# Storing the softmax reciprocals as rows, fixed bias places, scaling o in place, and other DMA queues in an encoder layer

## The chip, the cores and the metric

The kernel runs on one core of a Trainium2 chip. A core has five engines: TensorE (PE in the profile, with its weight loads as PEld), VectorE (DVE), ScalarE (ACT), GpSimd (POOL) and SyncE (SP), which only issues DMAs here. Each engine takes its instructions in order. SyncE and GpSimd each feed a DMA queue of their own (q1 and q0 in the profile), and both queues are served by the same 16 DMA engines. The metric is the time of one execution on the device in microseconds; less is better.

## The reference

One layer of a streaming encoder is computed for two groups of frames: a prompt of 1024 frames and 64 further frames of a running stream (the sample), which has 512 cached rows of keys and values. All is float32.

```
proj = rmsnorm(x, g_mix) @ w_in              # columns: cb cc ch | q k v | ga gb
cv   = causal depthwise conv, width 3, of cc*ch
ya   = (cb * cv) @ w_conv_out
o    = softmax(q k^T / 8 + bias, over the own chunk of 64 and the 8 before) @ v   # 8 heads of 64
yb   = o @ w_attn_out
x    = x + (sigmoid(ga)*ya + sigmoid(gb)*yb) @ w_out
x    = x + (silu(n @ w1) * (n @ w3)) @ w2    # n = rmsnorm(x, g_ffn)
y    = rmsnorm(x, g_final)
```

The outputs are y for both groups, the last two inputs of the convolution, and the key and value rows to be kept.

## The kernel before, in words

**Numbers.** A float32 operand is split into two parts (`split`, L119): ScalarE casts the high part (L121) and VectorE subtracts it (L122). A product is three matmuls, high by high, high by low and low by high. Large products use seven block products in place of eight (`run`, L218).

**Frames.** The 1088 frames are kept in two halves of 544: 512 prompt frames and 32 sample frames each. Attention works on tiles of 128 prompt frames (t = 0 to 7) and one tile of the 64 sample frames (t = 8).

**Normalization and v** (L337 to L506). Nine tiles of frames are loaded in the order of `ORDER` (sample first), normalized, turned on TensorE (L405) and multiplied with the weights of v. The loads of the first two tiles and of these weights stand on SP's queue. The row `gm` (L374) holds the gains of the norm, turned by TensorE and copied by ScalarE; no tile can be scaled (L391) without it. `put_v` splits v and stores it per head to `v_d`, on Pool's queue.

**Projection units** (L476 to L738). Each unit is 256 columns of `w_in`. The list `units` sets the order. A unit's results go to DRAM scratch: `q_d`, `k_d`, `gb_d`, and `u_d` for cb times the convolution. While the first units run, four tiles of cached keys and values are loaded, turned and stored (`cache_tile`, L666).

**Attention beside gates** (L742 to L972). The rest of ga and gb, 12 blocks of 128 columns in `GATES`, are plain products, cut in 4 pieces of 272 frames (`gate`, L751): 24 matmuls of 128x272 a piece. Each piece is copied by ScalarE into one of two buffers (L759) and stored (L760). Attention is a generator of 75 steps: a step does the scores of one tile (`scores`, L822), the turning of the tile two steps back (`transposed`) and, for every second tile, the values of the tile three steps back (`values`). After each gate piece `between` (L931) lets some steps run: `PER` of them on average. Pieces 0 and 1 of the first four gates run without attention. The constant `LAST` says how many gates are left when attention must be through. The instructions of one engine are ordered by the compiler's planner, which moves them by its own model of times, so the order on SP is not strictly that of the code.

For each head `head_load` (L766 to L789) loads keys, queries (two copies of each of two parts), values and a bias tile, about 3 MB. The bias tile is 128 by 640; two corners of it are set to -1e30 by VectorE after the load (L787, L788). In `softmax` one VectorE instruction adds the bias and finds the row's maximum (L795), and ScalarE takes the exponential with the row sum (L805). `combine` (L807) adds the two parts of the values and stores o, not yet divided by the row sum, to `o_d` (L816, L820) from `co`, which has two buffers. At t = 8 VectorE takes the reciprocals of a head's sums (L847, L848), and Pool stores them to `rc_d` (L850, L853) from a tile in which partition p holds the value of frame p of each tile:

```python
nc.gpsimd.dma_start(
    rc_d[h, e * HT : e * HT + 512].rearrange("(t p) -> p t", p=P), sm[:, 4 * e : 4 * e + 4]
)
```

**Merge** (L949 to L998). With the last gate, for each k of four, u and o are loaded, and rc is spread over the 64 partitions of its head; VectorE multiplies o by rc (L967) and `split` writes the operand `ob`. The tiles of o (`ol`) and rc have one buffer each. Then for each of 8 blocks of columns come ya and yb, the sigmoids, and the sum of both.

**The rest** (L1000 on): output projection, second norm, feed-forward part and final norm. The change touches nothing there.

Of the kernel before, what the change touches and what calls it, by code (L numbers as in the profile page):

```python
# [8 lines left out]
F32 = mybir.dt.float32  # L9
# [24 lines left out]
HN = HT // 2  # L34
KB = [2, 3, 3, 3]
C_CB, C_CC, C_CH, C_Q, C_K, C_V, C_GA, C_GB = 0, 512, 1024, 1536, 2048, 2560, 3072, 4096
PER = 2.1
LAST = 1


class Quarters:
# [23 lines left out]
def encoder_kernel(ctx: ExitStack, tc: tile.TileContext, ins, outs):  # L65
# [40 lines left out]
    def bias_rows(h, a, n):  # L106
        return spread(ins["bias_ext"][h, a : a + n], n)
# [226 lines left out]
    def bank1(tag, nm):  # L334
        return ps1.tile([P, 2, 512], F32, tag=tag, name=nm, bufs=2)

    def put_v(st, src, n, row):  # L337
        st = st.bitcast(F32R).rearrange("p (h l d) -> p h l d", h=NH, l=2)
        s = src.rearrange("p (h d) -> p h d", h=NH)
        split(st[:n, :, 0, :], st[:n, :, 1, :], s[:n])  # L340
        nc.gpsimd.dma_start(
            v_d[:, row : row + n, :].rearrange("h t e -> t h e"),
            st[:n].rearrange("p h l d -> p h (l d)").bitcast(F32),
        )
# [9 lines left out]
    wv_raw = [rpool.tile([P, 4, ATT], F32, tag="raw", name=f"wv{half}") for half in range(2)]  # L354

    def load_wv(k0):
        nc.sync.dma_start(
            wv_raw[k0 // 4][:, k0 % 4 : k0 % 4 + 2],
            w_in[k0 * P : (k0 + 2) * P, C_V : C_V + ATT].rearrange("(k p) n -> p k n", p=P),
        )  # L360

    load_x(ORDER[0])
    load_wv(0)
    load_x(ORDER[1])
    load_wv(2)
    load_wv(4)
    load_wv(6)
# [6 lines left out]
    act.activation(gm, gp, AF.Copy, scale=-0.5)  # L374

    wv = []

# [77 lines left out]
    def v_tile(i):  # L455
        t0, n = TT[i]
        pv = bank1("BD", f"pvv{i}")[:, 0]
        for k in range(KD):
            if i == 8:
                a, b = xs8[:, k, :TS], xs8[:, k, TS:]  # L460
            else:
                a, b = xn.at(0, k, column(i), P), xn.at(1, k, column(i), P)
            mm(pv[:n], a, wv[k][0], start=k == 0, stop=False)
            mm(pv[:n], a, wv[k][1], start=False, stop=False)
            mm(pv[:n], b, wv[k][0], start=False, stop=k == KD - 1)
        put_v(slot(VST, D), pv, n, t0 if t0 < TP else TP + CACHE)
        if t0 >= TP - CACHE:
            v32 = scr[:, SQ : SQ + ATT]
            act.copy(v32[:n], pv[:n])
            if t0 < TP:  # L470
                dst = outs["cache_v_prompt"][t0 - (TP - CACHE) : t0 - (TP - CACHE) + n]
            else:
                dst = outs["cache_v_sample"][CACHE - TS :]
            nc.gpsimd.dma_start(dst, v32[:n])

    units = []  # L476
    for nm, u in (
        ("q", 0), ("q", 1), ("k", 0), ("k", 1), ("cc", 0), ("ch", 0), ("cb", 0), ("cc", 1), ("ch", 1), ("cb", 1),
        ("gb", 0), ("gb", 1),
    ):  # L480
        base = {"q": C_Q, "k": C_K, "cc": C_CC, "ch": C_CH, "cb": C_CB, "gb": C_GB}[nm]
        units.append((nm, u, w_in[:, base + 2 * u * P : base + 2 * (u + 1) * P]))
# [183 lines left out]
    def cache_tile(i):  # L666
        ct = cts[i]
        a = 0 if i else TS
        row = i * P + a - TS
        for nm, o in (("k", 0), ("v", ATT)):  # L670
            nc.gpsimd.dma_start(outs[f"cache_{nm}_sample"][row : row + P - a], ct[a:, o : o + ATT])
        put_v(slot(CC, 2 * ATT), ct[:, ATT:], P, TP + i * P)
        pk = bank1("BD", f"ckp{i}")[:, 0]
        for hp in range(4):
            nc.tensor.transpose(pk[:, hp * P : (hp + 1) * P], ct[:, hp * P : (hp + 1) * P], ident)
        st = slot(CC, 2 * ATT).bitcast(F32R).rearrange("p (l a t) -> p l a t", l=2, a=4)
        split(st[:, 0], st[:, 1], pk.rearrange("p (a t) -> p a t", a=4))
# [73 lines left out]
    def gate(i, cs):  # L751
        g, m = GATES[i]
        dst = ga_d if g == "a" else gb_d
        for c in cs:
            o, n = PIECES[c]
            ps = pmm.tile([P, 512], F32, tag="mm", name=f"g{i}_{c}")
            product(ps[:, :n], gate_w[i], xn, o, n)
            st = st_pool.tile([P, HN], F32, tag="st", name=f"gst{i}_{c}")
            act.copy(st[:, :n], ps[:, :n])  # L759
            nc.sync.dma_start(dst[m * P : (m + 1) * P, o : o + n], st[:, :n])  # L760

    gate_w = {}

    heads, sums = {}, {}

    def head_load(h):  # L766
        k = hd_pool.tile([P, TP], F32R, tag="k", name=f"kd{h}")
        nc.sync.dma_start(k.bitcast(F32), k_d[h, :, :, :TP].rearrange("l d t -> (l d) t"))
        q = []
        for l in range(2):  # L770
            qq = hd_pool.tile([P, T], F32R, tag=f"q{l}", name=f"qd{h}_{l}")
            for j in range(2):
                nc.sync.dma_start(qq[j * HD : (j + 1) * HD].bitcast(F32), q_d[h, l])
            q.append(qq)
        ks = hd_pool.tile([P, CACHE + TS], F32R, tag="ks", name=f"ksd{h}", bufs=1)
        nc.sync.dma_start(ks.bitcast(F32), k_d[h, :, :, TP:].rearrange("l d t -> (l d) t"))
        v = hd_pool.tile([P, 8, P], F32R, tag="v", name=f"vd{h}")
        nc.sync.dma_start(v.bitcast(F32), v_d[h, :TP].rearrange("(b p) e -> p b e", p=P))
        vs = hd_pool.tile([P, 5, P], F32R, tag="vs", name=f"vsd{h}", bufs=1)
        nc.sync.dma_start(vs[:, :4].bitcast(F32), v_d[h, TP : TP + CACHE].rearrange("(b p) e -> p b e", p=P))  # L780
        nc.sync.dma_start(vs[:TS, 4].bitcast(F32), v_d[h, TP + CACHE :])
        b = hd_pool.tile([P, 640], F32, tag="b", name=f"bias{h}")
        nc.sync.dma_start(b[:, :384], bias_rows(h, 0, 384))
        nc.sync.dma_start(
            b[:, 384:], bias_d[h, 127 : 127 + P * 383].rearrange("(p n) -> p n", n=383)[:, :256]
        )
        vec.memset(b[HD:, :HD], NEG)  # L787
        vec.memset(b[:HD, 576:], NEG)  # L788
        heads[h] = (q, k, ks, v, vs, b)  # L789

    def softmax(s, ps, bias, sm, nm):
# [15 lines left out]
    def combine(h, pv, n, tok, nm):  # L807

        a = at_pool.tile([HD, 2, 256], F32, tag="cmb_a", name=f"ca{nm}", bufs=1)
        o = at_pool.tile([HD, 256], F32, tag="cmb_o", name=f"co{nm}")  # L810
        act.copy(a[:, :, :n], pv[HD:])
        vec.tensor_tensor(a[:, :, :n], pv[:HD], a[:, :, :n], op=ALU.add)
        vec.tensor_tensor(o[:, :n], a[:, 0, :n], a[:, 1, :n], op=ALU.add)
        if tok < TP:
            c = tok if tok < 512 else HT + tok - 512
            nc.sync.dma_start(o_d[h * HD : (h + 1) * HD, c : c + n], o[:, :n])  # L816
        else:
            for e in range(2):
                c = 512 + e * HT
                nc.sync.dma_start(o_d[h * HD : (h + 1) * HD, c : c + 32], o[:, 32 * e : 32 * e + 32])  # L820

    def scores(h, t):  # L822
# [14 lines left out]
        b0 = 640 - n if t < 8 else 0  # L837
        if t == 0:
            sums[h] = at_pool.tile([P, 9], F32, tag="sm", name=f"sm{h}")
        sm = sums[h]  # L840
        softmax(
            s[:r, :n], ps[:r, :, :w] if parts == 2 else ps[:r, 0, :w], bias[:r, b0 : b0 + n], sm[:r, t : t + 1],
            f"{h}_{t}",
        )
        if t == 8:

            vec.reciprocal(sm[:, :8], sm[:, :8])  # L847
            vec.reciprocal(sm[:TS, 8:], sm[:TS, 8:])  # L848
            for e in range(2):
                nc.gpsimd.dma_start(  # L850
                    rc_d[h, e * HT : e * HT + 512].rearrange("(t p) -> p t", p=P), sm[:, 4 * e : 4 * e + 4]
                )
                nc.gpsimd.dma_start(  # L853
                    rc_d[h, e * HT + 512 : e * HT + HT].rearrange("(p t) -> p t", t=1), sm[32 * e : 32 * e + 32, 8:]
                )
        return s

    pts = {}
# [1 line left out]
    def transposed(h, t, s):  # L860
        tp = patt.tile([P, 2, 512], F32, tag="att", name=f"t{h}_{t}").rearrange("p a b -> p (a b)")
        if t == 8:
# [6 lines left out]
            split(pt[:, 0, :4, :], pt[:, 1, :4, :], tp[:, : 4 * TS].rearrange("p (b t) -> p b t", t=TS))  # L869
            split(pt[:TS, 0, 4, :], pt[:TS, 1, 4, :], tp[:TS, 512 : 512 + TS])  # L870
            pts[h, 4] = pt
            return
        g, j = divmod(t, 2)
        if j == 0:
# [72 lines left out]
    for i in range(4, len(GATES)):  # L947
        gate_w[i] = next_w()
        if i == len(GATES) - LAST:  # L949
# [6 lines left out]
            mp = pg_stack.enter_context(tc.tile_pool(name="mgp", bufs=4, reuse_waits="tile"))  # L956
            for k in range(4):
                nc.sync.dma_start(u.t[:, :, k].bitcast(F32), u_d[k])
                t = mp.tile([P, T], F32, tag="ol", name=f"ol{k}", bufs=1)
                nc.sync.dma_start(t, o_d[k * P : (k + 1) * P])  # L960
                r = mp.tile([P, T], F32, tag="rc", name=f"rc{k}", bufs=1)
                for j in range(2):
                    src = rc_d[2 * k + j]
                    nc.sync.dma_start(
                        r[j * HD : (j + 1) * HD], bass.AP(tensor=src.tensor, offset=src.offset, ap=[[0, HD], [1, T]])
                    )
                vec.tensor_tensor(t, t, r, op=ALU.mult)  # L967
                split(ob.t[:, 0, k], ob.t[:, 1, k], t)
        for c in range(4):
            gate(i, (c,))  # L970
            between()
# [575 lines left out]
```

## Time and profile before

| | |
|---|---|
| median of 3 runs | 1606.53 us (1606.35 to 1609.5) |
| profiled execution | 1621.55 us, span 1619.6 us |
| busy in the span | PE 1505.9 us (93%), DVE 984.9 (61%), ACT 682.8 (42%), POOL 101.2 (6%) |
| DMA | 262.91 MB, mean 162 GB/s |
| instructions | 26436, of them 10178 matmuls |

The page cuts the span into 40 slices and gives each engine's busy share in tenths for each. Below it are the DMA queues, the chain of work that ended last, and groups of like instructions: line, engine, operation, tile written <- tiles read, shape, count, busy time, mean time of one, and the idle time ahead of them with what ended it. Tiles go by the names in the code, without buffer numbers. The other views answer for one stretch, one tile or one engine: who waited for whom, instructions in order of time, and busy times in windows.

### The profile page before, as it was taken

The numbers are of one execution on the slowest core, as the hardware profiler recorded it, in microseconds if no ns is written. First come the engines' busy times: TensorE is split into PE (matmuls) and PEld (weight loads), VectorE is DVE, ScalarE is ACT, GpSimd is POOL, SyncE is SP. The second block draws the span as 40 slices with busy tenths as digits, with TensorE's granted clock in tenths as the row PEclk, the third lists the DMA queues.
The fourth block names the chain that finished last, engine by engine and source line by source line (L and its number), as shares of the span: only waits on it lengthen the run. The fifth ranks groups of instructions, "written<-read, shape, count | busy, mean of one in ns | idle before, by whom it ended". The sixth has DMA issues, their size and how long they took to land.

```text
span 1619.6 us, 26436 instructions
## 1 busy us (share of the span) xinstructions
PE 1505.9 (93%) x10178; PEld 1408.2 (87%) x10178; DVE 984.9 (61%) x1865; ACT 682.8 (42%) x1382; POOL 101.2 (6%) x175
## 2 busy tenths in 40 slices
PE   6889999998889779779999899999999999899998
PEld 5789999998888778779988899999999999688886
DVE  6774466630655456356537966666666667856677
ACT  6543333331555445244315644444444445512133
POOL 1210000000001000000000001111101000000000
PEclk9999999999999899879999999999999999999999
DMA  6587654457667672564443234444343336876676
GB/s 206 165 237 196 191 44 156 75 173 221 133 133 128 122 151 75 184 199 142 149 144 124 87 115 144 147 147 147 134 147 136 133 132 226 309 230 216 227 263 206
DMA packets 169894, 262.91 MB, mean 162 GB/s; under 512 B 22592, under 2 KB 107720, under 8 KB 169640
## 3 DMA queue, kind: packets, MB, share of 16 engines
q1 hardware_dynamic: 151224, 201.01, 45.0%
q0 software_dynamic: 17392, 58.11, 10.0%
q8 instruction: 80, 1.31, 0.4%
q10 hardware_dynamic: 1152, 2.10, 0.4%
q14 instruction: 46, 0.38, 0.1%
HBM read 169.24 MB, written 91.92 MB: 161 GB/s over the span
## 4 chain that ended last, share of the span: by engine, by line
PE 65%; DMA 13%; issue 11%; DVE 5%; ACT 2%; POOL 1%; SPq 1%; another core or an unknown queue 0%; ACTq 0%; POOLq 0%; DVEq 0%
PE A L1464 6%; PE Ab L238 6%; PE Aa L238 6%; DMA o_d<-co 4%; PE D L1464 3%; PE Db L238 3%; PE Da L238 3%; PE B L1464 2%; PE g L302 2%; PE g L300 2%; PE g L301 2%; PE Bb L238 1%; PE Agb L238 1%; PE t L880 1%; PE Acc L238 1%
## 5 line engine op out<-in xcount | busy, mean ns | idle before, releaser
L1464 PE MATMUL A<-ring,ht 128*128 128x512 f32 x528 | 125.0, 390 | 3.9 <-ACT acc L1474 2.2
L1464 PEld LDWEIGHTS A<-ring,ht 128*128 128x128 f32 x528 | 98.7, 188 | 25.9 <-ACT acc L1474 3.5
L300 PE MATMUL g<-xn,whp 128*128 128x272 f32 x384 | 117.6, 306 | 1.0 <-ACT scr L523 1.0
L302 PE MATMUL g<-xn,wlp 128*128 128x272 f32 x384 | 115.1, 300 | 0.0
L301 PE MATMUL g<-xn,whp 128*128 128x272 f32 x384 | 114.4, 298 | 0.0
L121 ACT CAST ring<-w2r 128x512 fp32r<-128x512 f32 (+1 forms) x78 | 43.7, 588 | 104.1 <-PE A L1464 51.2
L121 ACT CAST hq<-sa 128x512 fp32r<-128x512 f32 x77 | 47.6, 619 | 88.9 <-DVE sa L1197 56.0
L300 PEld LDWEIGHTS g<-xn,whp 128*128 128x128 f32 x384 | 76.5, 199 | 1.9 <-ACT scr L523 1.2
L302 PEld LDWEIGHTS g<-xn,wlp 128*128 128x128 f32 x384 | 76.2, 199 | 0.8
L301 PEld LDWEIGHTS g<-xn,whp 128*128 128x128 f32 x384 | 76.4, 199 | 0.1
L122 DVE TENSOR_TENSOR hq<-sa,hq 128x512 fp32r<-128x512 f32 x77 | 53.1, 690 | 36.8 <-ACT hq L121 36.7
L795 DVE CUSTOM_DVE_ANT_0 p<-s,bias 128x640 f32<-128x640 f32 (+5 forms) x72 | 47.4, 660 | 34.4 <-PE s L836 30.2
L1185 POOL DMA_DIRECT2D h_d<-hq x77 | 41.0, 532 | 422.2 <-DVE hq L122 250.7
L238 PE MATMUL Aa<-tt,wha 128*128 128x272 f32 x352 | 60.4, 293 | 4.7 <-ACT tt L121 3.5
L805 ACT ACTIVATE p<-p,mx 128x640 f32<-128x640 f32 (+5 forms) x72 | 50.9, 707 | 32.5 <-DVE mx L795 30.9
L1464 PE MATMUL D<-ring,ht 128*128 128x512 f32 x264 | 62.9, 390 | 1.7 <-ACT acc L1474 1.7
L835 PE MATMUL s<-kd,qd 128*128 128x320 f32 (+2 forms) x96 | 33.3, 353 | 33.3 <-DVE mx L795 31.5
L122 DVE TENSOR_TENSOR wla<-rawa,wha 128x512 fp32r<-128x512 f32 x56 | 38.4, 687 | 42.3 <-ACT wha L121 42.3
L238 PE MATMUL Ab<-tt,whb 128*128 128x272 f32 x352 | 58.9, 289 | 1.6 <-ACT whb L121 1.6
L1464 PEld LDWEIGHTS D<-ring,ht 128*128 128x128 f32 x264 | 49.5, 188 | 12.4 <-ACT acc L1474 2.1
L238 PE MATMUL Ab<-mg,whb 128*128 128x272 f32 x352 | 58.4, 288 | 0.0
L238 PE MATMUL Aa<-mg,wha 128*128 128x272 f32 x352 | 58.3, 288 | 0.0
(512 smaller groups left out, 4384.3 us busy)
## 6 DMA issues: line engine op xcount, KB each, us to landing
h_d<-hq POOLq DMA_DIRECT2D x77, 512.0 KB
ht<-h_d SPq DMA_DIRECT2D x154, 256.0 KB, 3.5
rawa<-in_w_ff SPq DMA_DIRECT2D x11, 1024.0 KB, 6.1
rawb<-in_w_ff SPq DMA_DIRECT2D x11, 1024.0 KB
w2r<-in_w_ff SPq DMA_DIRECT2D x11, 1024.0 KB, 5.6
qd<-q_d SPq DMA_DIRECT2D x32, 272.0 KB, 13.1
v_d<-scr POOLq DMA_DIRECT2D x12, 512.0 KB
rawp<-in_w_in SPq DMA_DIRECT2D x6, 1024.0 KB, 5.3
```

The lines of the kernel that those rows point to most:

```text
L121: act.copy(hi, src)
L122: vec.tensor_tensor(lo, src, hi.bitcast(F32), op=ALU.subtract)
L238: mm(t[:, j, :HN], w[:, k, :], x[p][:, l, k, j * HN : (j + 1) * HN], start=p in (1, 2, 7) and k == 0 and n == 0, stop=k == 3 and n == 2, s ...
L300: mm(out, a, p, start=k == 0, stop=False)
L301: mm(out, a, q, start=False, stop=False)
L302: mm(out, b, p, start=False, stop=k == kt - 1)
L795: vec.tensor_tensor_reduce(out=s if len(ps.shape) == 2 else s.rearrange("p (a b) -> p a b", a=2), in0=ps, in1=bias if len(ps.shape) == 2 e ...
L805: act.activation(s, s, AF.Exp, bias=mx, scale=-1.0, accum_out=sm)
L835: mm(ps[:r, i, :w], q[0][:, qs], k[:, ksl], start=True, stop=False)
L880: nc.tensor.transpose(tp[:, i * P : (i + 1) * P], s[:, i * P : (i + 1) * P], ident)
L1185: nc.gpsimd.dma_start(h_d[p, c - 1], hq.rearrange("p i l t -> p (i l t)").bitcast(F32))
L1464: mm(t, ht[k][:, j, x], w[:, l], start=p in (1, 2, 7) and k == 0 and n == 0, stop=k == len(ks) - 1 and n == 2, skip_group_check=p in (6, 5 ...
```

## The change

- The reciprocals of a head are no longer stored at t = 8. When the sample tile is turned, one matmul turns the 128 by 9 tile of reciprocals to 9 rows in PSUM (a third use of the tag `att`), ScalarE copies them, and Pool stores rows of 128 to `rc_d`. Unused places of the sums are set to 1 by Pool.
- The bias tiles are two fixed places, masked once by Pool; a head's load leaves the masked corners out and becomes four DMAs in place of two.
- `co` has three buffers.
- In the merge all of u is loaded first, o is loaded into the place of its operand's high part, and rc has two buffers and takes the product.
- Attention runs at 2.35 steps a piece and is through before the last two gates.
- Gate pieces are stored by Pool, v rows of the cache by SP. The weights of v are loaded on Pool's queue, the second tile of frames ahead of them. VectorE in place of ScalarE writes `gm`.
- Unit gb0 stands between ch0 and cb0.

```diff
-PER = 2.1
-LAST = 1
+PER = 2.35
+LAST = 2
...
-    def put_v(st, src, n, row):
+    def put_v(st, src, n, row, queue):
...
-        nc.gpsimd.dma_start(
+        queue.dma_start(
...
     def load_wv(k0):
-        nc.sync.dma_start(
+        nc.gpsimd.dma_start(
...
     load_x(ORDER[0])
+    load_x(ORDER[1])
     load_wv(0)
-    load_x(ORDER[1])
...
-    act.activation(gm, gp, AF.Copy, scale=-0.5)
+    vec.tensor_scalar(gm, gp, -0.5, None, op0=ALU.mult)
...
-        put_v(slot(VST, D), pv, n, t0 if t0 < TP else TP + CACHE)
+        put_v(slot(VST, D), pv, n, t0 if t0 < TP else TP + CACHE, nc.gpsimd)
...
-        ("q", 0), ("q", 1), ("k", 0), ("k", 1), ("cc", 0), ("ch", 0), ("cb", 0), ("cc", 1), ("ch", 1), ("cb", 1),
-        ("gb", 0), ("gb", 1),
+        ("q", 0), ("q", 1), ("k", 0), ("k", 1), ("cc", 0), ("ch", 0), ("gb", 0), ("cb", 0), ("cc", 1), ("ch", 1),
+        ("cb", 1), ("gb", 1),
...
-        put_v(slot(CC, 2 * ATT), ct[:, ATT:], P, TP + i * P)
+        put_v(slot(CC, 2 * ATT), ct[:, ATT:], P, TP + i * P, nc.sync)
...
-            nc.sync.dma_start(dst[m * P : (m + 1) * P, o : o + n], st[:, :n])
+            nc.gpsimd.dma_start(dst[m * P : (m + 1) * P, o : o + n], st[:, :n])
...
+    bb = at_pool.tile([P, 2, 640], F32, name="bb", bufs=1)
+    for j in range(2):
+        nc.gpsimd.memset(bb[HD:, j, :HD], NEG)
+        nc.gpsimd.memset(bb[:HD, j, 576:], NEG)
...
-        b = hd_pool.tile([P, 640], F32, tag="b", name=f"bias{h}")
-        nc.sync.dma_start(b[:, :384], bias_rows(h, 0, 384))
-        nc.sync.dma_start(
-            b[:, 384:], bias_d[h, 127 : 127 + P * 383].rearrange("(p n) -> p n", n=383)[:, :256]
-        )
-        vec.memset(b[HD:, :HD], NEG)
-        vec.memset(b[:HD, 576:], NEG)
+        b = bb[:, h % 2]
+        near = bias_d[h, 127 : 127 + P * 383].rearrange("(p n) -> p n", n=383)
+        far = bias_rows(h, 0, 384)
+        nc.sync.dma_start(b[:HD, :384], far[:HD])
+        nc.sync.dma_start(b[HD:, HD:384], far[HD:, HD:])
+        nc.sync.dma_start(b[:HD, 384:576], near[:HD, :192])
+        nc.sync.dma_start(b[HD:, 384:], near[HD:, :256])
...
-        o = at_pool.tile([HD, 256], F32, tag="cmb_o", name=f"co{nm}")
+        o = at_pool.tile([HD, 256], F32, tag="cmb_o", name=f"co{nm}", bufs=3)
...
             sums[h] = at_pool.tile([P, 9], F32, tag="sm", name=f"sm{h}")
+            nc.gpsimd.memset(sums[h][HD:, 8:], 1.0)
...
-            vec.reciprocal(sm[:, :8], sm[:, :8])
-            vec.reciprocal(sm[:TS, 8:], sm[:TS, 8:])
-            for e in range(2):
-                nc.gpsimd.dma_start(
-                    rc_d[h, e * HT : e * HT + 512].rearrange("(t p) -> p t", p=P), sm[:, 4 * e : 4 * e + 4]
-                )
-                nc.gpsimd.dma_start(
-                    rc_d[h, e * HT + 512 : e * HT + HT].rearrange("(p t) -> p t", t=1), sm[32 * e : 32 * e + 32, 8:]
-                )
...
+            sm = sums.pop(h)
+            vec.reciprocal(sm, sm)
+            tr = patt.tile([P, 2, 512], F32, tag="att", name=f"rt{h}")[:9, 0, :P]
+            nc.tensor.transpose(tr, sm, ident)
+            rows = at_pool.tile([P, P], F32, tag="rows", name=f"rows{h}", bufs=1)[:9]
+            act.copy(rows, tr)
+            for e in range(2):
+                nc.gpsimd.dma_start(
+                    rc_d[h, e * HT : e * HT + 512].rearrange("(t p) -> t p", p=P), rows[4 * e : 4 * e + 4]
+                )
+                c = e * HT + 512
+                nc.gpsimd.dma_start(rc_d[h : h + 1, c : c + 32], rows[8:9, 32 * e : 32 * e + 32])
...
-                t = mp.tile([P, T], F32, tag="ol", name=f"ol{k}", bufs=1)
-                nc.sync.dma_start(t, o_d[k * P : (k + 1) * P])
-                r = mp.tile([P, T], F32, tag="rc", name=f"rc{k}", bufs=1)
+            for k in range(4):
+                o = ob.t[:, 0, k].bitcast(F32)
+                nc.sync.dma_start(o, o_d[k * P : (k + 1) * P])
+                r = mp.tile([P, T], F32, tag="rc", name=f"rc{k}", bufs=2)
...
-                vec.tensor_tensor(t, t, r, op=ALU.mult)
-                split(ob.t[:, 0, k], ob.t[:, 1, k], t)
+                vec.tensor_tensor(r, o, r, op=ALU.mult)
+                split(ob.t[:, 0, k], ob.t[:, 1, k], r)
```

More of the change, by code (lines that the diff above doesn't have):

```diff
@@ L844, in scores @@
         )
-        if t == 8:
-            vec.reciprocal(sm[:, :8], sm[:, :8])
-            vec.reciprocal(sm[:TS, 8:], sm[:TS, 8:])
-            for e in range(2):
-                nc.gpsimd.dma_start(
-                    rc_d[h, e * HT : e * HT + 512].rearrange("(t p) -> p t", p=P), sm[:, 4 * e : 4 * e + 4]
-                )
-                nc.gpsimd.dma_start(
-                    rc_d[h, e * HT + 512 : e * HT + HT].rearrange("(p t) -> p t", t=1), sm[32 * e : 32 * e + 32, 8:]
-                )
         return s
```

## The prediction

> **What bounds the kernel now.** I read the page first: the span, then the busy slices of TensorE and the clock granted to it.
>
> ```profile
> span 1619.6 us, 26436 instructions
> ...
> PE   6889999998889779779999899999999999899998
> ...
> PEclk9999999999999899879999999999999999999999
> ```
>
> A slice is 40.5 us. TensorE is at 9 almost everywhere, so the kernel is bound by TensorE's work, and only an idle stretch of TensorE is to be won. The low digits are slice 0 (the start), slices 13 and 14 (526 to 607 us, attention) and slices 16 and 17 (648 to 729 us, where the merge begins). Nearly all that the diff touches lies before slice 18; after it nothing changes. Next I read TensorE's waits (who waited for whom: total us, times, longest), then two rows of all engines' waits.
>
> ```profile
> PE s L835 <- DVE mx L795: 31.5, 7, 7.2
> PE yb L300 <- ACT ob L121: 19.2, 4, 5.5
> PE xt L405 <- DVE scr L391: 9.9, 5, 8.4
> PE t L880 <- DVE pt L122: 6.6, 8, 4.4
> ...
> PE Acb L238 <- DVE scr L533: 2.8, 1, 2.8
> ```
>
> ```profile
> DVE bias L787 <- DMA bias<-in_bias_ext: 43.8, 7, 21.8
> ...
> DVE co_s L813 <- DMA o_d<-co: 32.1, 7, 8.1
> ...
> ACT gst L759 <- DMA ga_d<-gst: 16.1, 1, 16.1
> ```
>
> The first row is attention: the scores wait for VectorE, seven times, about once a head. The second is the merge: yb waits for the scaled o. VectorE in turn is held by two things that are not arithmetic: the memset of a bias tile, which waits for that tile's load, and co_s, which waits until an earlier store to o_d frees its buffer. VectorE takes its work in order, so each of these stops softmax. One such stop, in time order:
>
> ```profile
> 469.22 0.22 DVE L813 TENSOR_TENSOR co_s<-ca_s 64x64 f32<-64x64 f32 x1 [5.95 <-DMA o_d<-co]
> ...
> 470.10 0.64 PE L835 MATMUL s<-kd,qd 128*128 128x320 f32 x1 [5.55 <-DVE mx L795]
> ```
>
> Why is a 64 KB store late? The view by windows shows it (busy us and instructions of PE, PEld, DVE, ACT, POOL; then granted clock, DMA share, GB/s):
>
> ```profile
> 456.00:460.00 4.00, 4.00 (x30) 3.45 (x29) 2.24 (x8) 2.41 (x8) 0.00 (x0) 1.00 1.14 102
> 460.00:464.00 4.00, 4.00 (x30) 3.69 (x29) 1.97 (x6) 2.37 (x7) 0.00 (x0) 1.00 0.91 38
> 464.00:468.00 4.00, 0.54 (x5) 0.32 (x3) 0.00 (x0) 0.20 (x1) 0.00 (x0) 1.00 0.70 58
> 468.00:472.00 4.00, 1.90 (x8) 1.86 (x9) 1.59 (x5) 0.81 (x2) 0.00 (x0) 0.54 0.94 254
> 472.00:476.00 4.00, 4.00 (x21) 3.90 (x21) 2.87 (x7) 2.39 (x5) 0.00 (x0) 0.61 0.62 144
> 667.00:670.00 3.00, 2.80 (x23) 2.59 (x22) 0.94 (x2) 1.24 (x2) 0.00 (x0) 1.00 1.02 419
> 386.00:663.00 277.00, 242.68 (x1669) 227.57 (x1668) 143.90 (x352) 142.20 (x329) 20.70 (x32) 0.93 0.61 121
> 663.00:703.00 40.00, 19.90 (x109) 18.30 (x108) 11.73 (x10) 8.47 (x12) 0.00 (x0) 0.71 0.82 262
> 720.00:740.00 20.00, 20.00 (x162) 20.00 (x161) 12.86 (x34) 10.86 (x30) 0.00 (x0) 1.00 0.50 143
> ```
>
> From 456 to 468 us the DMA engines are 70 to 114% busy and move 38 to 102 GB/s; at 667 us as busy a set moves 419. So for some 12 us they are full of something that carries no bytes. What had just been issued are the reciprocals of the row sums, two stores of 2 KB a head, each in pieces of 4 bytes (the number for frame p of tile t lies on partition p and goes to place 128t+p). From the view of DMA issues, and the tile's own:
>
> ```profile
> rc_d<-sm POOLq DMA_DIRECT2D x16, 2.0 KB
> ```
>
> ```profile
> L850 POOL DMA_DIRECT2D rc_d<-sm x16: 750/783/804, 418.3 to 648.8; - x16
> ```
>
> I take these stores as what clogs the engines, by time and order only. The stop also costs clock: after it the rows at 468 and 472 us show 0.54 and 0.61 granted.
>
> **The change part by part.** The sum is made against the profiled execution, 1621.55 us (span 1619.6 and 2 us around it). That is 15.0 us, 0.9%, above the median of 1606.53 (1606.35 to 1609.5); I carry the difference over unchanged, and come back to it in the range.
>
> *Attention, 386 to 663 us.* TensorE is busy 242.68 of 277, so 34.3 us are idle. The clock row says 0.93, so 19.4 us of full clock are missing in all. How much of that fell on work? In the 468 and 472 rows it is 4 × 0.46 + 4 × 0.39 = 3.4 us, of which the idle time up to 470.1 us holds 2.1 × 0.5 = 1.05; so some 70% is on work, 13.6 us. Together 47.9 us could go. The change takes away both holders of VectorE: reciprocals go out as 512-byte rows (8 pieces a head and two of 128 bytes instead of 1088 of 4), a third co buffer lets one more store be late, and the bias tiles are masked once, so no memset waits for a load. It also takes the 48 gate stores off SP, where o's stores and the head loads stood behind them. What is late next: the head loads themselves, some 3 MB a head by the code, on the same SP queue as o's stores, and TensorE's wait for VectorE and ScalarE, now packed closer (75 steps in 32 gate pieces at 2.35 where it was 36 at 2.1). VectorE is at 143.90 of 277, 52%, so rate is no limit, but waits like t on pt (6.6 us) stay or grow. I take 70%: −33.5 us, with bounds of −17 and −47.9.
>
> *Start of the merge, 663 to 703 us.* Idle 40 − 19.90 = 20.1; missing clock 40 × 0.29 = 11.6, half of it on work by the busy share: 6. Together 26.1. Before, each quarter of o waits for the one before to be multiplied and split out of the single buffer; after, u and o need no such buffer and rc has two. The code loads 4 × 1.11 MB of u, 4 × 0.56 of o and 8 × 0.28 of rc, 8.9 MB: 21.3 us at the 419 GB/s of the 667 row, 34 at the mean of 262. I take 28, plus some 3 for the last multiply and split. What covers it: the work that TensorE did there already, 19.9 us, and one more gate, 4 pieces of 24 matmuls at 20/162 = 0.123 us, 11.9 us. 31.8 against 31: just covered. I leave 4 us for the first yb: −22, bounds −8 (the loads take 34 us and start late) and −26.1.
> [...]
>
> *Start of the kernel.* Two rows of the timeline bracket the wait of 8.36 us:
>
> ```profile
> 6.97 0.15 DVE L159 SCALAR_TENSOR_TENSOR scr<-scr 64x1 f32<-64x1 f32 x1
> ...
> 10.65 1.02 ACT L374 ACTIVATE scr<-gm_rows 128x1024 f32<-128x1024 f32 x1
> ...
> 13.04 1.11 PE L405 MATMUL xt<-ident,scr 64*128 64x64 f32 x8 [8.36 <-DVE scr L391]
> ```
>
> The frame factors are there at 7.12 us; the scale row gm comes at 11.67, because ScalarE, in order, first squares the second tile. On VectorE it can be there before 7.12: up to 4.5 us earlier. The v weights move to Pool's queue behind the second x tile and then end the wait sooner: −3, bounds 0 and −4.5.
>
> *The order of the projection units.* gb0 stands between ch0 and cb0 and gives the convolution time; of the waits it can reach, the largest row is Acb's 2.8 us. −2, bounds +3 (another unit meets the late buffer) and −3, with what clock follows.
>
> *Added.* A head's reciprocals are turned by one matmul into a third use of the two attention PSUM buffers and copied by ScalarE. Behind the turning matmul stand the next head's scores, behind the copy the next exponentials, and behind Pool's store the gate stores. Between the 0.22 us of a small VectorE instruction and the 0.64 of a slow matmul (rows above), 0.3 a head: +2.4 over 8, bounds 0 and 5.
>
> *Gate stores on Pool.* Two pieces of the chain in time order are stores issued by Pool, with their time to landing:
>
> ```profile
> 25.42 5.14 DMA out_cache_v_sample<-scr
> ...
> 60.63 7.68 DMA out_cache_v_prompt<-scr
> ```
>
> Two buffers hold a gate piece, so a piece can't come oftener than half a landing: 2.6 to 3.8 us, against 24 × 0.123 = 2.96 of matmuls. In attention pieces are far apart and nothing is lost. In the last 8 pieces it costs 0 to 0.9 each, 0 to 7; ya's matmuls cover part. +1, as the lower row costs nothing.
>
> *At nothing.* Two more bias loads a head: SP's issues, hidden as long as SP is ahead of attention; if not, 1.6 us a head (two at the 783 ns of L850, the nearest row). The cache's v stores move from Pool to SP, behind q and k stores and ahead of weight loads: between −3 and +5, taken as 0, since the DMA engines do the same work.
>
> Sum: −33.5 − 22 − 3 − 2 + 2.4 + 1 = −57.1. That makes 1564.4 profiled and 1606.5 − 57.1 = 1549.4, say **1549 us**.
>
> **The rivals.** *The head loads clog, not the reciprocals* (chance 0.15). For it: they are issued in the same microseconds, on SP's own queue, and a store queues behind them. Against: 38 GB/s is no load at work. Then attention keeps two thirds of its stops, the third buffer saves the rest: −16 in place of −33.5, 1567 us.
>
> *The merge stays bound by its loads* (0.08): they begin only after attention's last store, take 34 us and the last gate store is late. −8 in place of −22: 1563 us.
>
> *Pool's stores become the bound: slower* (0.04). ScalarE copies a gate piece only into a free buffer; while it waits, exponentials and operand casts queue behind it. Now 48 pieces take 341 us (362 to 703), 7.1 us each; with two buffers the stage is longer than before once a landing passes 14.2 us. At the 16.1 us of the ACT gst row it takes 48 × 8.05 = 386 us: 1652. Against: Pool's landings above, of 5.14 and 7.68 us.
> [...]
>
> **How the numbers follow.** The forecast has 0.73. If the 15 us by which the profiled execution is longer lie in the very stops that go, the gain is 42 and the time 1564. With all terms at their far ends it is 1527. The range **1528 to 1580** takes in the forecast with its bounds and the first two rivals, and leaves out 1 to 2 in 10. About 0.2%, 3 us, can be told from no change; faster 0.94, same 0.02 (gains and the bounds of the added costs cancel), slower 0.04, the third rival.
>
> **What would show it.** Right: in the windows after each head's reciprocals no stretch of full DMA engines at under 100 GB/s; co_s and bias gone from VectorE's longest waits; "PE s on DVE mx" under 10 us in place of 31.5; the clock in attention at 0.97 or more; "PE yb on ACT ob" under 5 us in place of 19.2; the first xt wait near 4 us. Wrong: the low-rate windows remain with the 4-byte pieces gone (first rival), yb waits over 10 us (second), or ScalarE's gst waiting on its store over 20 us in all (third).

## The result, and the profile after

| | before | after |
|---|---|---|
| median (runs, lowest to highest) | 1606.44 us (4, 1606.01 to 1609.5) | 1555.18 us (4, 1552.32 to 1557.29) |
| profiled execution (span) | 1621.55 us (1619.6) | 1552.32 us (1550.5) |
| TensorE busy | 1505.9 us (93%) | 1487.9 us (96%) |

The ratio is 0.9676, with a 95% interval of 0.9653 to 0.9698: faster, inside the range of 1528 to 1580, 6 us above the 1549 forecast. The span is 69.1 us shorter: 51.1 us of idle TensorE (113.7 to 62.6, span less busy time) and 18.0 us of its busy time, though it does 8 matmuls more. These 18 us I put down to the clock, whose mean rose from 0.969 to 0.988: the 384 matmuls of the gates' first product (L300) took 306 ns each before and 297 after. The page of after, first the span, then TensorE's busy tenths and granted clock:

```profile
span 1550.5 us, 26487 instructions
...
PE   6998999999999999799998999999999999899997
...
PEclk9999999999999999899999999999999999999999
```

A slice is now 38.8 us. Slices 9 to 14, attention, read 9 without a gap. What is left low is the start, slice 3 (116 to 155 us, the projection units), slice 16 (620 to 659 us, the merge), and places behind it that the change does not touch. TensorE's waits in after (who waited for whom: total us, times, longest):

```profile
PE xt L405 <- DVE scr L391: 9.9, 3, 8.9
PE yb L300 <- ACT ob L121: 5.4, 3, 2.7
PE Ak L238 <- ACT whk L121: 4.0, 1, 4.0
...
PE g L300 <- ACT gst L759: 2.6, 2, 1.8
...
PE yb L301 <- DVE ob L122: 2.4, 3, 0.9
...
PE yb L300 <- DVE ga L997: 1.7, 1, 1.7
...
PE s L841 <- DVE mx L801: 1.2, 3, 0.7
```

The wait of the scores for VectorE, 31.5 us before, is 1.2 us. The wait of Ak was 1.1 us before and is 4.0, and the first xt wait has not become shorter (8.9 us, 8.4 before). The windows of after (span, busy us and instructions of PE, PEld, DVE, ACT, POOL; granted clock, DMA share, GB/s):

```profile
443.00:447.00 4.00, 4.00 (x29) 3.64 (x28) 2.46 (x9) 2.35 (x7) 0.57 (x1) 1.00 0.81 223
447.00:451.00 4.00, 4.00 (x32) 3.91 (x32) 2.80 (x6) 2.71 (x6) 0.55 (x1) 1.00 0.68 176
451.00:455.00 4.00, 4.00 (x32) 3.85 (x31) 2.59 (x5) 3.09 (x7) 0.00 (x0) 1.00 0.63 215
455.00:459.00 4.00, 3.91 (x32) 3.69 (x31) 3.80 (x9) 2.63 (x6) 0.54 (x1) 1.00 0.51 139
386.00:600.00 214.00, 210.87 (x1516) 196.07 (x1516) 139.92 (x328) 140.04 (x329) 36.52 (x75) 0.99 0.55 149
613.00:633.00 20.00, 10.55 (x64) 8.66 (x62) 10.51 (x10) 7.07 (x10) 1.08 (x2) 0.77 0.86 235
...
633.00:653.00 20.00, 19.93 (x140) 19.51 (x141) 14.67 (x36) 11.13 (x30) 0.00 (x0) 0.89 0.53 161
```

In attention the idle time fell from 34.3 to 3.1 us and the clock rose from 0.93 to 0.99. The first four rows follow the second head's reciprocals, which Pool issued at 440.40 to 442.42 us: the DMA engines are 51 to 81% busy and move 139 to 223 GB/s, where full engines moved 38 to 102 before. In the merge 9.5 of 40 us are idle, where it was 20.1.

### The profile page after: what moved, and what is told of

It reads as the page before. It is cut to its first block, busy times and chain, and to the rows that moved or that the text cites. A ratio compares the mean times of both kernels' runs of the same rounds, so it can differ in the third digit from the quotient of the medians.

```text
span 1550.5 us, 26487 instructions
## 1 busy us (share of the span) xinstructions
PE 1487.9 (96%) x10186; PEld 1389.1 (90%) x10186; DVE 982.5 (63%) x1842; ACT 682.6 (44%) x1389; POOL 123.4 (8%) x235
## 4 chain that ended last, share of the span: by engine, by line
PE 73%; issue 9%; DMA 7%; DVE 6%; ACT 3%; POOL 1%; SPq 0%; ACTq 0%; POOLq 0%; DVEq 0%
PE Ab L238 8%; PE Aa L238 7%; PE A L1474 6%; PE Db L238 4%; PE Da L238 4%; PE D L1474 2%; PE Bb L238 2%; PE g L302 2%; PE Ba L238 2%; PE g L301 2%; PE g L300 2%; PE B L1474 2%; PE Acb L238 2%; PE Ak L238 1%; PE t L889 1%
## 5 line engine op out<-in xcount | busy, mean ns | idle before, releaser
L300 PE MATMUL g<-xn,whp 128*128 128x272 f32 x384 | 113.9, 297 | 3.6 <-ACT gst L759 2.6
L301 PE MATMUL g<-xn,whp 128*128 128x272 f32 x384 | 111.3, 290 | 0.0
L801 DVE CUSTOM_DVE_ANT_0 p<-s,bb 128x640 f32<-128x640 f32 (+5 forms) x72 | 47.5, 661 | 52.9 <-DMA vd<-v_d 29.9
L300 PEld LDWEIGHTS g<-xn,whp 128*128 128x128 f32 x384 | 72.8, 190 | 4.8 <-ACT gst L759 3.0
L302 PEld LDWEIGHTS g<-xn,wlp 128*128 128x128 f32 x384 | 72.6, 189 | 0.7
L301 PEld LDWEIGHTS g<-xn,whp 128*128 128x128 f32 x384 | 72.8, 190 | 0.4
L122 DVE TENSOR_TENSOR ring<-w2r,ring 128x512 fp32r<-128x512 f32 (+1 forms) x78 | 49.0, 647 | 16.5 <-ACT ring L121 16.3
L121 ACT CAST wha<-rawa 128x512 fp32r<-128x512 f32 x56 | 34.8, 622 | 53.6 <-PE Ab L238 36.6
```

What stands on the lines that cost most here:

```text
L121: act.copy(hi, src)
L122: vec.tensor_tensor(lo, src, hi.bitcast(F32), op=ALU.subtract)
L300: mm(out, a, p, start=k == 0, stop=False)
L301: mm(out, a, q, start=False, stop=False)
L302: mm(out, b, p, start=False, stop=k == kt - 1)
L801: vec.tensor_tensor_reduce(out=s if len(ps.shape) == 2 else s.rearrange("p (a b) -> p a b", a=2), in0=ps, in1=bias if len(ps.shape) == 2 e ...
```

## The experiments

The theory to begin with was the prediction's: the 4-byte stores of the reciprocals clog the DMA engines, o's store is late, and VectorE stands behind it. The main rival was the first of the prediction, that the head loads clog and the reciprocals only stand nearby. "Before" and "after" are the two kernels. There were three groups of runs, each with the kernel before on the same chip: its medians were 1616.71 us (11 runs; rows, holders, merge, after without the rows), 1617.11 (23 runs; each holder alone, gb0, the pace) and 1616.87 (9 runs; the rest). Ratios are to these, with a 95% interval.

**Before, with the rows alone.** The reciprocals are turned and stored as rows as in the diff; all else is before.

```diff
-                nc.gpsimd.dma_start(
-                    rc_d[h, e * HT : e * HT + 512].rearrange("(t p) -> p t", p=P), sm[:, 4 * e : 4 * e + 4]
-                )
...
+                nc.gpsimd.dma_start(
+                    rc_d[h, e * HT : e * HT + 512].rearrange("(t p) -> t p", p=P), rows[4 * e : 4 * e + 4]
+                )
```

> The kernel before with the reciprocals turned and stored as rows, nothing else. Theory (the 4-byte pieces fill the DMA engines, o's store lands late, VectorE stops): co_s waits of 32.1 us fall under 8, 'PE s on DVE mx' from 31.5 to under 12, no stretch of full DMA engines under 100 GB/s after a head; the profiled execution 25 to 35 us shorter, the timed one 15 to 30 shorter (ratio 0.981 to 0.991). Rival (the head loads fill the engines): co_s and PE's waits stay over 25 us, ratio 0.997 to 1.003. On the difference between profile and median (15 us before): if the profile lengthens the 4-byte pieces themselves it falls under 4 us here; if it comes from anything else it stays near 15.

Measured: 1579.34 us (1577.39 to 1582.24), 0.9768 (0.9743 to 0.9793). TensorE's and VectorE's waits in this kernel:

```profile
PE yb L300 <- ACT ob L121: 15.7, 4, 4.6
...
PE s L835 <- DVE mx L795: 8.6, 7, 4.2
...
DVE bias L787 <- DMA bias<-in_bias_ext: 44.5, 8, 21.5
```

The scores wait 8.6 us in place of 31.5, and VectorE's wait at co_s, 32.1 us before, is gone. The head loads were left as they were, so the rival falls: the pieces are what clogs. All of attention says so: cut into stretches of 4 us, it has 9 to 11 in which the DMA engines are 60% busy or more and move under 110 GB/s in each profiled kernel with the pieces that I cut so (before, the next three below, and after without the rows), and none with the rows (this one, after in both its executions, gate stores on SP, and the faster version's first). The gain is larger than the 0.981 to 0.991 expected. The memset of the bias still waits 44.5 us, but 21.5 of these are the first head's, at attention's start, and the other seven are 3.3 us on average, most of which TensorE does not feel (8.6 us in all, 4.2 of them one stop at attention's start).

**Before, with the two holders taken away.** Bias tiles in fixed places and a third `co` buffer; the reciprocals still go out in pieces of 4 bytes.

```diff
-        b = hd_pool.tile([P, 640], F32, tag="b", name=f"bias{h}")
+        b = bb[:, h % 2]
...
-        o = at_pool.tile([HD, 256], F32, tag="cmb_o", name=f"co{nm}")
+        o = at_pool.tile([HD, 256], F32, tag="cmb_o", name=f"co{nm}", bufs=3)
```

> The kernel before with the fixed bias places and the third buffer of co alone; the 4-byte pieces stay. Theory: the low-rate stretches of the DMA engines stay; VectorE's waits on the bias load go and co_s's get shorter by one buffer, so a third to a half of the stops in attention remains; ratio 0.985 to 0.995, the profile still some 15 us above the median. Rival (head loads): these two edits carry the gain of attention, ratio 0.975 to 0.985, and PE's wait for VectorE under 8 us.

Measured: 1576.22 us (1572.58 to 1580.76), 0.9758 (0.9732 to 0.9785). Its waits and its windows:

```profile
PE yb L300 <- ACT ob L121: 18.3, 4, 5.3
...
PE s L841 <- DVE mx L801: 6.3, 6, 4.4
...
DVE co L819 <- DMA o_d<-co: 2.1, 2, 1.5
```

```profile
443.00:447.00 4.00, 4.00 (x30) 3.81 (x30) 2.46 (x6) 3.05 (x7) 1.87 (x3) 1.00 1.07 390
447.00:451.00 4.00, 4.00 (x33) 3.65 (x32) 3.02 (x9) 2.44 (x8) 0.72 (x2) 1.00 1.52 204
451.00:455.00 4.00, 4.00 (x28) 3.65 (x28) 1.91 (x6) 1.97 (x6) 0.00 (x0) 1.00 0.54 27
455.00:459.00 4.00, 4.00 (x31) 3.76 (x30) 1.97 (x6) 1.89 (x5) 0.00 (x0) 1.00 0.83 68
...
386.00:614.00 228.00, 225.10 (x1642) 211.02 (x1642) 141.73 (x335) 139.00 (x320) 20.69 (x32) 1.00 0.72 143
```

The clog is there, behind stores that Pool issued at 445.1 to 447.7 us: from 451 to 459 us the engines move 27 and 68 GB/s while 54 and 83% busy. TensorE is busy 4.00 of 4.00 us throughout, and 225.10 of 228 in the whole of attention, at a clock of 1.00; 4.4 of the 6.3 us that the scores still wait are the one stop at attention's start. So in this kernel the clog alone costs next to nothing, and the pieces alone were not the cause: a stop took the clog and an instruction of VectorE that waits for a DMA. The theory's range of 0.985 to 0.995 was missed. The ratio and the 6.3 us are what the rival had named, but not by its mechanism: it had the head loads clog, and with the rows they don't.

**Each holder alone.** First the third `co` buffer alone, then the fixed bias places alone, both on before.

> The kernel before with three co buffers in place of two, nothing else: 4-byte pieces and memsets stay. Theory A (the stop is VectorE waiting at co_s for a free buffer, and the late store is all of it): attention loses its stops, ratio 0.974 to 0.982, co_s's wait under 5 us. Theory B (the memset behind the bias load is as much of it): co_s's wait goes, bias' wait of 43.8 us stays or grows into its place, ratio 0.985 to 0.995.

> The kernel before with the fixed bias places alone: 4-byte pieces and two co buffers stay. Theory A: most stops stay, since co_s still waits for late stores, ratio 0.990 to 1.000. Theory B: half of them go, ratio 0.985 to 0.990, and VectorE starts on the first head some 14 us earlier without a gain for PE, which has gates to do there.

Measured: 1621.99 us (1613.84 to 1625.31), 1.0019 (1.0001 to 1.0037), for the buffer; 1605.70 us (1600.11 to 1614.39), 0.9926 (0.9897 to 0.9955), for the bias. The waits and one stop of the kernel with the third buffer:

```profile
PE s L835 <- DVE mx L795: 28.9, 6, 8.1
...
DVE bias L787 <- DMA bias<-in_bias_ext: 71.4, 8, 21.7
```

```profile
538.15 0.11 DVE L787 MEMSET bias<- 64x64 f32 x1 [8.64 <-DMA bias<-in_bias_ext]
...
539.51 0.64 PE L835 MATMUL s<-kd,qd 128*128 128x320 f32 x1 [8.09 <-DVE mx L795]
```

The wait at co_s is gone, and the memset, next in VectorE's order, waits 71.4 us where it waited 43.8. The bias load stands behind the same pieces (without the longest, the memset waits 7.1 us a head here and 3.3 with the rows). The stop moved to the next holder. That is theory B's mechanism without the gain it had left (0.985 to 0.995). With the bias alone it is the other way round:

```profile
PE s L841 <- DVE mx L801: 23.7, 8, 6.2
...
DVE co_s L819 <- DMA o_d<-co: 30.6, 8, 6.6
```

Alone the two give +0.2% and -0.7%, together -2.4%: either holder left in place keeps most of the stops.

**After, without the rows.** The converse: all of the diff but the pieces of 4 bytes stay.

> The changed kernel with the reciprocals again stored in 4-byte pieces, all else kept. Theory: low-rate stretches return after each head; with three co buffers and no memset behind a load some of it is absorbed: 5 to 25 us over the changed kernel, ratio to before 0.970 to 0.983, and the profile longer than the median by 8 us or more. Rival (head loads): no difference from the changed kernel, ratio 0.966 to 0.970, profile and median within 4 us.

Measured: 1565.69 us (1563.14 to 1571.41), 0.969 (0.9665 to 0.9714). After itself had 0.9676, and 0.9636 in another group (below); so beside the other edits the rows are worth between nothing and half a per cent, though alone they give 2.3%. The ratio lies in the rival's range, again without its mechanism. The clog is felt a little here:

```profile
386.00:608.00 222.00, 211.42 (x1492) 195.62 (x1492) 141.13 (x340) 138.33 (x320) 39.48 (x67) 0.98 0.73 138
```

10.6 us of attention are idle where after has 3.1. TensorE's waits at t are 9.7 us (1.6 in after), and ScalarE waits 58.2 us for its gate pieces to be stored (35.4 in after). The gate stores are now on Pool's queue, with the pieces; that ScalarE is a third holder in this way is argued, from one execution.

**Before, with the merge and the pace of attention** (`PER`, `LAST`, loads of u first, o in its operand's place).

> The kernel before with the merge's edit alone: u first, o in its operand's place, two rc buffers, attention through before the last two gates at 2.35 steps a piece. Theory: 'PE yb on ACT ob' from 19.2 us to under 6, the stops of attention unchanged; 15 to 26 us less, ratio 0.984 to 0.991. Rival (the merge is bound by its loads, 8.9 MB): yb still waits over 10 us, ratio 0.992 to 0.997.

Measured: 1602.63 us (1600.15 to 1606.06), 0.9914 (0.9892 to 0.9935), some 14 us.

```profile
PE s L835 <- DVE mx L795: 18.9, 8, 4.4
PE t L880 <- DVE pt L122: 11.2, 7, 5.0
...
PE yb L300 <- ACT ob L121: 6.3, 3, 2.5
```

yb waits 6.3 us for ob in place of 19.2. The scores' waits fall to 18.9 as well and those of t grow from 6.6 to 11.2: the closer pace of attention moves the stops, and these 14 us are not the merge's alone. The ratio lies at the edge between the theory and the rival, and the 6.3 us just over the theory's mark of 6.

**Before, with gb0 between ch0 and cb0.**

```diff
-        ("gb", 0), ("gb", 1),
+        ("q", 0), ("q", 1), ("k", 0), ("k", 1), ("cc", 0), ("ch", 0), ("gb", 0), ("cb", 0), ("cc", 1), ("ch", 1),
```

> The kernel before with unit gb0 moved between ch0 and cb0, nothing else. Theory (the new place gives the convolution and the load of the next unit's weights time, and is the whole of the 7.8 us that the changed kernel's units gain by their end): the last unit ends 6 to 9 us earlier, ratio 0.994 to 0.997. Rival (the gain comes from the v stores and loads moved to other queues): the units end within 2 us of before, ratio 0.998 to 1.002.

Measured: 1610.34 us (1606.41 to 1616.35), 0.9964 (0.9946 to 0.9981): 3 to 9 us, as expected. The wait that it was put down to did not go: Acb waits 3.4 us here, for ScalarE's cast of its weights, and waited 2.8 for a sum by VectorE (L533) before. Where the gain arises stays open.

**After again, and after with one edit undone.** On one chip: after unedited; the gate stores back on SP's queue; and the start as before (v weights on SP's queue, tiles in the old order, `gm` by ScalarE, v rows of the cache stored by Pool).

> The changed kernel once more, unedited, so that the other three kernels of this group can be set against it on one chip. The earlier groups gave the kernel before 1616.7 and 1617.1 us where the first comparison gave 1606.4; if that is the chip and not the kernel, the ratio is still 0.966 to 0.970. If the gain depended on the chip, it would lie outside.

> The changed kernel with the 48 gate stores back on SP's queue. Theory (the stops of attention were the two holders of VectorE and the 4-byte pieces, and both are gone without this edit): ratio 0.966 to 0.970, no more than 0.002 from the changed kernel, and PE s on DVE mx stays under 5 us. Rival (SP's queue, with the gate stores ahead of o's stores and head loads, was itself a cause): waits of TensorE for VectorE in attention of 10 us or more and a ratio of 0.973 or more.

> The changed kernel with its first 60 us undone: v weights on SP's queue, the tiles in the old order, gm written by ScalarE, v rows of the cache stored by Pool. Theory (the new start is worth nothing, because ScalarE's first cast waits for the v weights on Pool's queue and delays the square of the first tile): within 0.002 of the changed kernel, first xt wait 8 to 9 us. Rival (the start is worth the 3 us of the prediction and lost them by chance): 0.002 or more slower.

| | median us | ratio |
|---|---|---|
| after | 1558.05 (1553.65 to 1560.64) | 0.9636 (0.9606 to 0.9666) |
| gate stores on SP | 1563.5 (1559.97 to 1564.19) | 0.9668 (0.964 to 0.9697) |
| start as before | 1550.49 (1548.92 to 1554.72) | 0.9594 (0.9566 to 0.9623) |

After's own ratio is below the 0.966 to 0.970 expected of it, its interval reaches in; its time is 3 us above that of the first comparison, and it is the kernel before that was 10 us slower. The gate stores on SP cost 5 us (the ranges of the two hardly touch, the intervals of the ratios overlap): more than the theory's bound, less than the rival's. Their landing is shorter there, and still the kernel is slower. First the DMA issues (KB each, median us to landing) of after in this group and of the kernel with the stores on SP, then, in time order, the first gate store of that kernel and its one long wait in attention:

```profile
ga_d<-gst POOLq DMA_DIRECT2D x32, 136.0 KB, 4.0
```

```profile
ga_d<-gst SPq DMA_DIRECT2D x32, 136.0 KB, 2.4
```

```profile
380.62 0.37 SPq L760 DMA_DIRECT2D ga_d<-gst  x1
...
385.00 0.69 PE L841 MATMUL s<-kd,qd 128*128 128x384 f32 x1 [4.70 <-DVE mx L801]
```

It is at attention's start, when the first head's tiles load, and does not come back: not the recurring stop of before. A stop of 4.1 to 4.7 us stands there in all eight profiled executions with gate stores on SP, before among them, and in none of the six with them on Pool. It is not that head 0's loads stand behind gate stores. It is the other way round: on SP the first gate store is issued behind them, at 380.62 us, 19.3 us after the first gate matmul; on Pool it goes out after 8.7 us. Between 377 and 385 us TensorE does no gate matmul, and its scores, which begin at 378.0 us in place of 390.0, wait for the loads. That the two full buffers of gate pieces hold the gates up is argued from this order, not tried.

The new start gains nothing and is more likely worse than the old one, against both the theory and the rival. The instructions of after in this group and of the kernel with the old start, in time order (start us, us, [idle before, and what ended it]; SPq is SP issuing a DMA):

```profile
6.42 0.62 ACT L121 CAST whv<-wv 128x512 fp32r<-128x512 f32 x1 [4.17 <-DMA wv<-in_w_in]
6.94 1.05 ACT L389 ACTIVATE scr<-scr 64x1024 f32<-64x1024 f32 x1
...
10.72 1.22 DVE L374 TENSOR_SCALAR scr<-gm_rows 128x1024 f32<-128x1024 f32 x1
...
99.27 1.41 SPq L341 DMA_DIRECT2D v_d<-scr  x1
...
125.66 0.60 SPq L178 DMA_DIRECT2D rawk<-in_w_in  x1
```

```profile
4.92 1.06 ACT L389 ACTIVATE scr<-scr 64x1024 f32<-64x1024 f32 x1 [2.68 <-DMA scr<-in_x_sample]
...
10.52 1.02 ACT L374 ACTIVATE scr<-gm_rows 128x1024 f32<-128x1024 f32 x1
...
97.11 1.13 SPq L178 DMA_DIRECT2D rawk<-in_w_in  x1
```

Two things are seen. At 5 us ScalarE stands at a cast of the v weights, which wait for Pool's queue, and squares the first tile 2 us later than with the old start; VectorE, with small steps of both tiles first, writes `gm` at 10.72 us, no sooner than ScalarE did at 10.52. And the first half of the k weights is issued on SP at 125.66 us in place of 97.11, now behind stores of q, k and v's cache rows: the Ak wait of 4.0 us. Which of the four edits moved it in the planner's order was not tried. These two are worth some 3 us (first xt wait 8.7 us against 8.3, Ak 4.0 against 1.1) of the 7.6 between the medians; the rest is not found. Single traces can't settle it: the gates begin at 354.4 and 360.3 us in the two executions of after, and at 355.8 with the old start.

**A faster version.** After with attention through before the last three gates (`PER = 2.7`, `LAST = 3`), first alone, then with the old start too.

```diff
-PER = 2.35
-LAST = 2
+PER = 2.7
+LAST = 3
```

> The changed kernel with attention through before the last three gates, at 2.7 steps a piece (28 pieces for 75 steps). Theory (the rest of yb's wait, 9.5 us with its missing clock, is cover that lacks): yb's waits under 3 us, 5 to 10 us less than the changed kernel, ratio 0.961 to 0.965. Rival (attention, packed closer, waits for VectorE and ScalarE itself): PE's waits in attention grow by 5 us or more, ratio 0.967 to 0.972.

> The changed kernel with attention at 2.7 steps a piece and through before the last three gates, and with the old start. The first edit alone gave 0.9548. Theory (the start is worth nothing): 0.953 to 0.957. If the old start is better than the new one because ScalarE's first square comes 2 us sooner: 0.951 to 0.953.

Measured: 1545.52 us (1541.32 to 1547.19), 0.9548 (0.9525 to 0.9572), and 1538.55 us (1538.14 to 1539.51), 0.9519 (0.9493 to 0.9546). The first is below the 0.961 to 0.965 expected, the second in the range of the better old start. The second was in the group of the table: 19.5 us under after on its chip, 12 of these by the pace (1550.49 to 1538.55). Its windows:

```profile
613.00:633.00 20.00, 18.19 (x131) 17.74 (x131) 14.64 (x29) 13.03 (x29) 0.54 (x1) 0.91 0.82 245
633.00:653.00 20.00, 20.00 (x162) 20.00 (x161) 14.72 (x37) 9.92 (x27) 0.00 (x0) 1.00 0.60 183
```

The 9.5 us that TensorE lost in the merge of after are down to 1.8, and its wait for ob is gone.

## Why the prediction was right, point by point

**Attention (-33.5, bounds -17 and -47.9): too little, by half of the mechanism.** From the first gate matmul to the last, which takes in attention, the profiled kernels take 306.3 us before and 258.9 after: -47.4, where the forecast with the added turn and the gate stores has -30.1. Some 4 us of it lie ahead of 386 us, in the stop at attention's start, which the prediction's window leaves out. The stores did clog, and undoing them alone gave 37.4 us. But the prediction put the stop down to them, as though the third buffer and the fixed bias were extras. Undoing only those two gave 40.5 us with the clog still there. The stop is a product of two things, so the gains of its parts don't add (37.4 and 40.5; on top of the rest of the diff the rows gave 0 to 8 us; rows and holders without the rest were not run), and half of the second cure is little (+0.2% and -0.7%). The step that failed is "I take 70%": idle time fell by 31.2 of 34.3 us, and most of the lost clock came back with it. The records do not count the pieces one by one (128 packets on Pool's queue from 456 to 468 us of before), but the cost of these stores is there (engines 54 to 114% busy at 27 to 102 GB/s behind them); by that alone the rows would be the cure, and the kernel with the holders removed shows that a cure is to be had with the strided stores left in.

**Merge (-22, bounds -8 and -26.1): right mechanism, too much.** yb's three waits are 9.5 us (5.4, 2.4 and 1.7), 7.8 of them for ob, in place of the 4 that were left to it, and the idle time fell by 10.6. From the last gate matmul to the first of the output projection the profiled kernels take 125.6 us before and 111.5 after, -14.1. The step that failed is "31.8 against 31: just covered". With one gate more as cover the wait for ob is gone, and with the closer pace that goes with it this is worth 12 us.

**Start (-3, bounds 0 and -4.5): no gain, and the wrong sign as far as it shows.** Undoing these edits is faster by 7.6 us of median; the intervals of the two ratios just overlap. The step "On VectorE it can be there before 7.12" took the frame factors where the old order had them; the new order puts a cast that waits for a slower load ahead of them on ScalarE. The moved stores "taken as 0" have the wait of Ak beside them, up from 1.1 to 4.0 us: inside their bounds of -3 and +5, towards the end that was not taken.

**Order of the units (-2): -3 to -9**, the right sign at or past the far bound of -3, and not by the wait of Acb that the term was taken from. **Added turn (+2.4, 0 to 5):** not to be told apart; the rows as a whole cost nothing that shows. **Gate stores on Pool (+1, 0 to 7): wrong sign**, 5 us gained, with a stop at attention's start that goes. The prediction had the head loads behind the gate stores on SP; at that stop the gate stores stood behind the loads. The sign named for the third rival came true without the rival: ScalarE waited 24.3 us on ga_d and 11.1 on gb_d, over the 20 that were set, and TensorE for ScalarE's copies 2.6 us in all. The threshold should have been put on TensorE's wait.

**The sum and the profiled run.** The sum of -57.1 stands beside -69.2 between the two profiled executions, -51.3 between the medians of the first comparison and -58.8 in the later group. That it is so near the last is in part luck: against the two profiled executions, on which it was made, attention was put 17 us too low and the merge 8 too high, and ahead of the gates, where -5 was forecast, they differ by -8.0, much of which may be spread (354.4 and 360.3 us, above). The far ends add up to -81.5, which is 1525 and not 1527. The 15 us by which the profiled run of before was above its median were carried over, and were not there in after (2.9 us below its median). In 43 further runs of before the time was 1610.53 to 1623.61 us, so the profiled 1621.55 was an ordinary one and the 1606 to 1609.5 of the first comparison were low. That the profiler lengthens the pieces is refuted: the kernel with the holders removed keeps them and was profiled at 1572.58 us, below its median of 1576.22. Why four runs were low stays open.

**Rivals.** The first fell with the rows alone. The second named the wait that was left, yb's 9.5 us, just under its mark of 10; the idle time that went, 10.6 us, is more than the 8 it allowed. The third did not come: Pool's landings of 4.0 us are far below 14.2. Of the six signs named for being right four came; the wait for ob (5.4 us, under 5 was named) and the first xt wait (8.9, near 4 was named) did not.

## What to carry to other kernels

When an in-order engine is stopped by a late transfer, list every instruction on it that waits for the same queue before taking one away: the next one takes over the stop (here the memset's wait went from 43.8 to 71.4 us), and a trial of one edit makes it look worth little or nothing. Either all holders go or what clogs the queue goes; here both were worth little more than one. An edit "at nothing" on a DMA queue is priced by what is issued behind it: with the new start a weight load went out 28.6 us later.

## What the runs showed of the hardware that was not expected

A head's 1088 pieces of 4 bytes by the code, 4.4 KB in all, held the DMA engines for 8 to 12 us at 27 to 102 GB/s, for SP's queue too, though Pool's queue issued them. The view of queues (packets, MB, share of 16 engines) of before from 456 to 468 us shows where the time is:

```profile
q1 hardware_dynamic: 390, 0.79, 90.4%
q0 software_dynamic: 128, 0.00, 1.1%
```

Nearly all of it is in SP's packets (q1), which take 0.45 us each on average at 2.0 KB; from 443 to 455 us of after 3012 of them fill 63.6%, 0.04 us each at 0.7 KB. So by the records it is not the pieces themselves that fill the engines: behind them the other queue's packets last some four times as long for their size. A store of 136 KB landed in 2.4 us from SP and 4.0 us from Pool, and the kernel with the slower landing was the faster; on SP beside the pieces, in before, it took 4.3. The clock that stops had cost was worth some 18.0 us of busy time, as far as all of that is clock. After the 5.55 us stop of before 0.54 and 0.61 were granted, over 4 us each. The merge of after shows 0.77 from 613 to 633 us as well, where the longest wait is 2.7 us, but TensorE is idle for 9.3 of the 13 us from 620 on. At the start the clock row can't be trusted: it reads 1.00 from 5 to 30 us of after, which holds a wait of 8.9 us, while matmuls of one shape run slowly there at first:

```profile
21.98 0.63 PE L464 MATMUL pvv<-wlv,xs 128*64 128x512 f32 x1
...
23.21 0.39 PE L464 MATMUL pvv<-wlv,xs 128*64 128x512 f32 x1
```

They take 0.63 us from 15.82 to 22.4 us, one each 0.43 us, and 0.39 to 0.40 from 23.21 on, one each 0.23 us. So TensorE ran slow behind that wait too.
